# Fixed experts' round: the gather and the products taken by halves of the channels, and the order in which its weight slots are handed on

## The chip, the cores and the metric

One core of a Trainium2 chip runs the whole program. The metric is the device time of one launch, in microseconds (us); lower is better. The kernel before takes 1513.57 us, the median of three runs.

## The reference, cut to what matters

Two layers of a decoder with 512 tokens of 1024 channels. Each layer has a dense part (projections, three token mixers, output projection, LayerNorm) and then a mixture of 32 experts, of which each token uses two:

```python
for l in range(DEPTH):                      # DEPTH = 2
    ...                                     # token mixers, projection, layer_norm
    ffn = hierarchical_moe(x, ...)
    x = layer_norm(ALPHA * x + ffn, ...)

def run_block(args):                        # rows of one expert
    rows, e = args
    xb = x_pad[rows]
    hdn = silu(xb @ w_gate[e]) * (xb @ w_up[e])     # 1024 -> 512
    return hdn @ w_down[e]                          # 512 -> 1024
```

Every expert has three matrices of 2 MB in f32 ("gate", "up", "down"), so a layer reads 192 MB of expert weights.

## The kernel before

**Rounds.** In `moe` (from line 1312) the experts are taken in 13 rounds of 128 token slots. Round 0 is the *fixed* round: experts 0 and 16 of the kernel's numbering, 64 slots each, known before the routing. Rounds 1 to 12 hold two or three of the other 30 experts each, sorted by how many tokens they got, so their weights can be loaded only after the routing.

**A round on TensorE (PE).** `gather` (line 1320) builds the tokens of a round, channels on the partitions: the activations are multiplied by a matrix of ones and zeros (token to slot), in 16 matmuls for a *quarter*, that is for two of the eight blocks of 128 channels (line 1330). ACT (line 1341) and DVE (line 1339) copy one block each from PSUM to `xg`, with gain and bias. With n = 1 it builds one round, with n = 2 two rounds at a time. `hidden` (line 1364) multiplies the eight blocks k = 0 to 7 of `xg` by "gate" and "up" (line 1370); it can call *fillers*, other work put between its products, after every odd k. `act` (lines 1382, 1383) applies silu on ACT and the product on DVE, `turn` (lines 1389, 1390) transposes the result, `down` (line 1401) multiplies it by "down". `gated` (lines 1411, 1412) weighs the rows, `spread` (lines 1419, 1424, 1426) adds them to the tokens.

**The masks.** `gating`, `gating_all` and `tokens` (lines 1241 to 1284) compute each token's weights and slots on DVE, with two exponentials on ACT. `gates(r)` (line 1295) makes round r's matrix on DVE in 11 instructions: eight of line 1302, one of line 1306, and two (lines 1307, 1308) that write the ones and zeros into `fa` and an f16 copy, which `gather` reads. There are two places for them, for odd and for even rounds; the fixed round's lie in the place of round 1. `by_slot(r)` transposes the weights of round r on TensorE (line 1352, four transposes); DVE reads the result twice (lines 1354, 1355). For round 0 the weights come from a product on POOL (line 1599).

**Slots and the weight stream.** Weights lie in SBUF slots of 1 MB, half a matrix each: half 0 holds the channel blocks 0 to 3 of "gate" or "up", half 1 the blocks 4 to 7. `drop` (line 363) returns the slots of one or more matrices to the free list: first the half 0 of each matrix named, then the half 1 of each. `feed` (line 319) takes the next loads of a fixed order, puts each in the next free slot and issues it on SyncE (SP), line 357. SyncE works through its program in order, so it stands at a load until TensorE has read the slot's last contents, with all later loads behind it.

**Order.** From line 1590 on, PE, SP, DVE, ACT and POOL run in the order in which the program is written. Around the change it is, per layer: `feed` (five slots are free), the gather of the fixed round, gating and token counts, `gates(1)`, the products of the fixed round with `by_slot(0)` as the fourth filler, `feed`, `gates(2)`, `counts`, `act`, half the gather of rounds 1 and 2, `turn`, the other half, `by_slot(1)`, `down` of the fixed round. The products of the fixed round go half by half already: k = 0 to 3 of "gate", k = 0 to 3 of "up", then k = 4 to 7 of each. Its slots come back matrix by matrix: "gate" half 0, "gate" half 1, "up" half 0, "up" half 1 (two slots each).

Of the kernel before, what the change touches and what calls it, by code (L numbers as in the profile page):

```python
# [48 lines left out]
def rounds():  # L49

    kinds = list(KINDS)
    caps = [c for k in kinds for c in SIZES[k]]
    assert len(caps) == NF

    order = sorted(range(NF), key=lambda n: -caps[n])
    place = {n: j for j, n in enumerate(order)}
    r, n = [], 0
    for k in kinds:
        at, members = 0, []
        for c in SIZES[k]:  # L60
            members.append((place[n], at, at + c))
            at += c
            n += 1
        r.append(members)
    return r


ROUNDS = rounds()
# [4 lines left out]
def columns(members):  # L73

    w = 64 if all((b - a) % 64 == 0 for _, a, b in members) else 32
    return [(e, c, c + w) for e, (_, a, b) in enumerate(members) for c in range(a, b, w)]
# [86 lines left out]
class Trunk:  # L163
# [1147 lines left out]
    def moe(self, l):  # L1311
# [4 lines left out]
        xg = flat(f[:, 0:4, :]).rearrange("p (k s) -> p k s", k=8)  # L1316
# [3 lines left out]
        def gather(quarters=range(4), n=2):  # L1320

            w = 128 * n
            for kk in quarters:
                ps = self.t()
                for j in range(2):
                    k = 2 * kk + j
                    i = 0
                    for src, one in ((x1h, oh), (x1l, self.oh16)):
                        for t in range(NT):
                            nc.tensor.matmul(  # L1330
                                ps[:, w * j : w * j + w], src[:, k, 128 * t : 128 * t + 128],
                                one[:, 0:n, t, :], start=(i == 0), stop=(i == 2 * NT - 1),
                            )
                            i += 1
                for j in range(2):
                    k = 2 * kk + j
                    src = ps[:, w * j : w * j + w]
                    if j:
                        nc.vector.tensor_scalar(xg[:, k, 0:w], src, gain(k), bias(k), OP.mult, OP.add)  # L1339
                    else:  # L1340
                        nc.scalar.activation(xg[:, k, 0:w], src, AF.Identity, bias=bias(k), scale=gain(k))  # L1341

        def gate_of(r):
            return self.sm.tile([128, 1], F32, tag="gv", name="gv")

        def by_slot(r):

            gv = gate_of(r)
            gt = self.gt[:, (r - 1) % 2, :]
            ps = self.t()  # L1350
            for t in range(NT):
                nc.tensor.transpose(ps[:, 128 * t : 128 * t + 128], gt[:, 128 * t : 128 * t + 128], self.ident)
            oT = fa[:, 2 + r % 2, :]
            nc.vector.tensor_scalar(oT, ps, 0.0, None, OP.is_gt)
            nc.vector.tensor_reduce(gv, ps, AX.X, OP.add)
            return oT, gv

        def members(r):
            return len(ROUNDS[r - 1]) if r else len(FIXED)

        def weights(r, *names):
            return [self.loaded[(l, n, r, e)] for n in names for e in range(members(r))]

        def hidden(pss, w, xs, blocks, fill=(), parts=((0, 8),)):

            fill = list(fill)
            for m, part in [(m, part) for part in parts for m in range(len(w))]:
                for k in range(*part):
                    for e, a, b in blocks:
                        nc.tensor.matmul(  # L1370
                            pss[m][a:b, :], xs[:, k, a:b], w[m][e][:, k, :],
                            start=(k == 0), stop=(k == 7),
                        )
                    if k % 2 == 1 and fill:
                        fill.pop(0)()
# [52 lines left out]
        halves = [(0, 0, 64), (1, 64, 128)]  # L1428
# [113 lines left out]
        def release(r, *names):  # L1542
            for n in names:
                self.drop(*((l, n, r, e) for e in range(members(r))))

        def first(r, fill=(), keep=0):

            pss = [self.g(), self.g()]
            a = (r - 1) % 2 if r else 0
            xs = xg[:, :, 128 * a : 128 * a + 128]  # L1550
            if r:
                for m, n in enumerate(("gate", "up")):
                    if m:
                        self.feed()
                    hidden(pss[m:], [weights(r, n)], xs, columns(ROUNDS[r - 1]), fill[4 * m : 4 * m + 4])
                    release(r, n)
            else:
                w = [weights(r, n) for n in ("gate", "up")]
                hidden(pss, w, xs, halves, fill, ((0, 4), (4, 8)))
                release(r, "gate", "up")  # L1560
            if keep == 1:
                spare.append(self.free.pop())
            held = [self.free.pop() for _ in range(4 if keep == 4 else 0)]
            self.feed()
            self.free.extend(held)
            return pss
# [10 lines left out]
        def spreads(r, oT, y):  # L1577
            s = 1.0 if r else ALPHA
            return [lambda t=t, hf=hf: spread(oT, y[hf], t, hf, s) for t, hf in every]
# [10 lines left out]
        with self.manual(ET.PE, ET.SP):  # L1590

            self.known = l
            self.feed()
            gather(n=1)
            self.gating()
            self.gating_all()
            oh0 = oh[:, 0, :, :].bitcast(F32)
            gt0 = self.gt[:, 1, :].rearrange("p (t s) -> p t s", t=NT)
            nc.gpsimd.tensor_tensor(
                out=gt0, in0=oh0, in1=self.Gp.unsqueeze(2).broadcast_to([128, NT, 128]), op=OP.mult  # L1600
            )
            self.tokens()
            self.gates(1)
            nxt = []
            pss = first(0, [lambda: None] * 3 + [lambda: nxt.extend(by_slot(0))])
            self.gates(2)
            self.counts()
            nc.gpsimd.tensor_copy(self.cnt[:, 64:96], self.perm)
            h = act(pss)
            self.fb = self.half("y", FR, "Y")[0]  # L1610
            gather((0, 1))
            turn(h, hT)
            gather((2, 3))
            oT, gv = nxt
            nxt = by_slot(1)
            steps = spreads(0, oT, second(0, gv))

            for r in range(1, NR + 1):
                last = r == NR
                more = r % 2 == 0 and not last  # L1620
                counts = (0, 2, 0, 2, 0, 2, 0, 2)
                if row_steps:
                    counts = (0, 3, 0, 3, 0, 3, 0, 3)
                    steps = [f for n, st in enumerate(row_steps) for f in (*steps[2 * n : 2 * n + 2], st)]
                    row_steps = []
                if more:
                    self.gates(r + 1)
                    self.gates(r + 2)
                some, rest = several(steps, counts)
                h = act(first(r, some, 1 if r == NR - 2 else 4 if r == SLOW else 0))  # L1630
                oT, gv = nxt
                for step in rest:
                    step()
                if more:
                    gather((0, 1))
                elif not last:
                    nxt = by_slot(r + 1)
                turn(h, hT)
                if more:
                    gather((2, 3))  # L1640
                    nxt = by_slot(r + 1)
                if last:

                    nc.scalar.activation(f[:, 6, 0:1], self.eps, AF.Sqrt)
                if r == NR - 2:

                    tags = (self.x1t, *spare)
                    self.EF = [self.take(n, ty, t) for n, ty, t in (("E", F32, self.mht), ("qg", FR, tags))]
                    tabs, row_steps = lnrows()
                if r == SLOW:  # L1650
                    slow()
                    self.feed()
                if not last:
                    steps = spreads(r, oT, second(r, gv))
# [4 lines left out]
        def finish(t, hf):  # L1659
# [4 lines left out]
        fill = [  # L1664
            lambda: gated(pss[0], gv, 0),
            lambda: [finish(t, 0) for t in (0, 1)],
            lambda: [finish(t, 0) for t in (2, 3)],
        ]
        wl = self.loaded[(l, "last")].t
        n = 4 // members(NR)  # L1670
        w = lambda e, hf, j: wl[(4 * hf + j) // n][:, n * e + j % n, :]
        pss = [self.g(), self.g()]
# [163 lines left out]
```

## Time and profile before

| | |
|---|---|
| median of three runs | 1513.57 us (1512.85 to 1513.63) |
| the profiled execution's own time | 1514.36 us |
| its span (first to last instruction) | 1512.7 us |
| PE busy | 1362.2 us, 90% |
| DVE busy | 689.1 us, 46% |
| ACT busy | 395.2 us, 26% |
| POOL busy | 153.1 us, 10% |
| read from HBM | 441.45 MB, 293 GB/s over the span |

How to read it: busy times are averages over unlike stages, so the share of the whole span says little of one stage. Times in the rows are microseconds from the start of the span. A row of the timeline gives the start, the length from the first to the last of the merged instructions, the engine, the line of the kernel, the operation, what it writes and reads, its shape, and how many instructions were merged; in square brackets, if the engine stood idle before it, for how long and what ended that. A row of busy times by stretch gives the stretch, its length, the busy time of PE, PEld (weight loads into the array), DVE, ACT and POOL with their counts of instructions, then the granted TensorE clock (1.00 is 2.4 GHz, 0.50 is 1.2 GHz), the share of the DMA engines that was busy, and GB/s.

### The profile page before, as it was taken

To read this page: it belongs to the slowest core of one execution; us is meant where nothing else is said; L and a number is where in the kernel's file an instruction comes from. 1 tells how busy PE (TensorE), PEld (TensorE's weight loads), DVE (VectorE), ACT (ScalarE), POOL (GpSimd) and SP (SyncE) were. 2 spreads that over 40 slices of the span, in tenths; PEclk is the share of its full clock that TensorE was granted. 3 is DMA by queue.
4 is the path that set the end of the run, shared out by engine and by line. 5 is a ranking of instruction groups with operands and counts; after the bars stand their busy time and mean duration, and the time that the engine had idled before them with its cause. 6 is when DMAs were issued, how large, how long until landed. Compare 5 with 4: busy or idle time off the path is not lost. (4 is left out here: it accounts for less than half of the span.)

```text
span 1512.7 us, 22662 instructions
## 1 busy us (share of the span) xinstructions
PE 1362.2 (90%) x8836; PEld 755.1 (50%) x8837; DVE 689.1 (46%) x1540; ACT 395.2 (26%) x720; POOL 153.1 (10%) x188
## 2 busy tenths in 40 slices
PE   8999997899998988999699998979999989889994
PEld 7876576534343434343378665866343424343431
DVE  4347758524423242422553676585344242424225
ACT  5446544111010101011364555341110101010112
POOL 1112205100000000000141221050000000000001
PEclk9999999899999999999899998988999999999997
DMA  9410250799999999999911025408999999999994
GB/s 346 143 56 1 102 205 28 306 381 420 420 419 422 420 421 412 420 422 412 382 65 59 1 82 189 149 29 321 389 420 420 419 421 421 421 413 421 420 408 166
DMA packets 84550, 445.15 MB, mean 294 GB/s; under 512 B 8080, under 2 KB 14352, under 8 KB 36816
## 3 DMA queue, kind: packets, MB, share of 16 engines
q1 hardware_dynamic: 83184, 440.15, 72.5%
q0 software_dynamic: 960, 2.90, 0.6%
q8 instruction: 74, 1.21, 0.3%
q10 hardware_dynamic: 288, 0.52, 0.1%
q14 instruction: 44, 0.36, 0.1%
HBM read 441.45 MB, written 2.10 MB: 293 GB/s over the span
## 5 line engine op out<-in xcount | busy, mean ns | idle before, releaser
L1370 PE MATMUL g<-w,f 128*32 128x512 f32 (+1 forms) x3072 | 399.6, 595 | 13.7 <-DMA w<-expert_w_up 9.4
L1370 PEld LDWEIGHTS g<-w,f 128*32 128x32 f32 (+1 forms) x3072 | 120.8, 112 | 248.1 <-issue 202.4
L1401 PE MATMUL g<-w,f 128*32 128x512 f32 (+1 forms) x1536 | 211.6, 653 | 29.2 <-ACT f L1390 10.1
L1424 DVE TENSOR_TENSOR X<-X,s 128x512 f32<-128x512 f32 x176 | 113.0, 683 | 256.7 <-PE s L1419 256.7
L1401 PEld LDWEIGHTS g<-w,f 128*32 128x32 f32 (+1 forms) x1536 | 58.3, 121 | 161.7 <-issue 131.2
L1412 DVE SCALAR_TENSOR_TENSOR y<-g,gv,y 128x512 fp32r<-128x512 f32 x52 | 38.9, 750 | 212.1 <-ACT y L1411 209.8
L1419 PE MATMUL s<-y,fa 128*128 128x512 f32 x416 | 126.7, 425 | 6.4 <-DVE X L1424 3.5
L1419 PEld LDWEIGHTS s<-y,fa 128*128 128x128 f32 x416 | 70.1, 189 | 103.8 <-issue 71.9
L1411 ACT ACTIVATE y<-g,gv 128x512 fp32r<-128x512 f32 x52 | 35.5, 687 | 215.7 <-PE g L1401 215.7
L1330 PE MATMUL t<-fa,mh 128*128 128x256 f32 (+1 forms) x448 | 79.0, 298 | 8.9 <-ACT f L1390 8.8
L1341 ACT ACTIVATE f<-t,pp 128x256 f32<-128x256 f32 (+1 forms) x56 | 30.7, 549 | 206.7 <-PE t L1330 206.7
L1339 DVE TENSOR_SCALAR f<-t,pp 128x256 f32<-128x256 f32 (+1 forms) x56 | 29.4, 525 | 93.1 <-ACT f L1341 93.1
L1330 PEld LDWEIGHTS t<-fa,mh 128*128 128x128 f32 x448 | 61.3, 191 | 15.4 <-ACT f L1390 11.7
L1330 PE MATMUL t<-f,x1l 128*128 128x256 f16 (+1 forms) x448 | 64.9, 267 | 0.0
L1382 ACT ACTIVATE f<-g 128x512 f32<-128x512 f32 x26 | 15.6, 599 | 183.1 <-PE g L1370 183.1
L1530 POOL DMA_DIRECT2D rows<-ln_gain x2 | 1.1, 548 | 614.2 <-DMA w<-expert_w_gate 307.2
L1390 ACT COPY f<-t 128x512 f32<-128x512 f32 x26 | 15.2, 585 | 167.7 <-PE t L1389 167.7
L404 POOL TENSOR_TENSOR X<-X,f 128x512 f32<-128x512 f32 x32 | 40.5, 1296 | 87.9 <-DVE x1l L948 82.4
L404 POOL TENSOR_TENSOR X<-X,E 128x512 f32<-128x512 f32 x11 | 16.3, 1486 | 306.2 <-ACT X L1696 154.6
L701 ACT ACTIVATE f<-f,nm 128x128 f32<-128x128 f32 (+3 forms) x64 | 35.7, 558 | 43.7 <-POOL nm L700 42.9
L371 DVE TENSOR_TENSOR fa<-w,fa 128x512 fp32r<-128x512 f32 (+1 forms) x36 | 31.3, 877 | 32.0 <-ACT fa L370 31.9
L700 POOL TENSOR_SCALAR nm<-mx 128x1 f32<-128x1 f32 x64 | 22.3, 352 | 180.6 <-DVE mx L697 119.0
(338 smaller groups left out, 2165.5 us busy)
## 6 DMA issues: line engine op xcount, KB each, us to landing
w<-expert_w_gate SPq DMA_DIRECT2D x128, 1024.0 KB, 19.8
w<-expert_w_up SPq DMA_DIRECT2D x128, 1024.0 KB, 19.8
w<-expert_w_down SPq DMA_DIRECT2D x116, 1024.0 KB, 19.8
w<-w_in SPq DMA_DIRECT2D x20, 1024.0 KB, 13.6
w<-expert_w_down SPq DMA_DIRECT2D x48, 256.0 KB, 5.3
w<-w_out SPq DMA_DIRECT2D x8, 1024.0 KB, 5.3
X<-x SPq DMA_DIRECT2D x4, 512.0 KB, 5.9
w<-w_in SPq DMA_DIRECT2D x4, 512.0 KB, 8.2
```

The costliest lines, as they stand in the source:

```text
L371: self.nc.vector.tensor_sub(lo, src, hi.bitcast(F32))
L404: e.tensor_tensor(out=x, in0=x, in1=row[:, 512 * h : 512 * h + 512], op=op)
L701: nc.scalar.activation(p, p, AF.Exp, bias=nm, scale=0.125, accum_out=den)
L1330: nc.tensor.matmul(ps[:, w * j : w * j + w], src[:, k, 128 * t : 128 * t + 128], one[:, 0:n, t, :], start=(i == 0), stop=(i == 2 * NT - 1),)
L1339: nc.vector.tensor_scalar(xg[:, k, 0:w], src, gain(k), bias(k), OP.mult, OP.add)
L1341: nc.scalar.activation(xg[:, k, 0:w], src, AF.Identity, bias=bias(k), scale=gain(k))
L1370: nc.tensor.matmul(pss[m][a:b, :], xs[:, k, a:b], w[m][e][:, k, :], start=(k == 0), stop=(k == 7),)
L1401: nc.tensor.matmul(pss[hf][a:b, :], hT[:, 128 * j + a : 128 * j + b], part(e, hf, j), start=(j == 0), stop=(j == 3),)
L1411: nc.scalar.mul(yh, ps, gv)
L1412: nc.vector.scalar_tensor_tensor(yl, ps, gv, yh.bitcast(F32), OP.mult, OP.subtract)
L1419: nc.tensor.matmul(ps, oT[:, 128 * t : 128 * t + 128], y[q], start=(q == 0), stop=(q == 1))
L1424: nc.vector.tensor_add(x, x, ps)
```

## The change

The fixed round is begun by halves of the channels. The first two quarters of its gather are followed at once by the products of blocks 0 to 3 (`start`, first call). The gating and the token counts follow, then the other two quarters, `gates(1)`, and the products of blocks 4 to 7 (`start`, second call), with `by_slot(0)` as the third filler of that call. One `drop` of all four matrices returns the slots as "gate" half 0, "up" half 0, "gate" half 1, "up" half 1. `first` now serves rounds 1 to 12 alone.

```diff
+        def start(pss, part, fill=()):
+
+            w = [weights(0, n) for n in ("gate", "up")]
+            hidden(pss, w, xg[:, :, 0:128], halves, fill, (part,))
+
         def first(r, fill=(), keep=0):
 
             pss = [self.g(), self.g()]
-            a = (r - 1) % 2 if r else 0
+            a = (r - 1) % 2
             xs = xg[:, :, 128 * a : 128 * a + 128]
-            if r:
-                for m, n in enumerate(("gate", "up")):
-                    if m:
-                        self.feed()
-                    hidden(pss[m:], [weights(r, n)], xs, columns(ROUNDS[r - 1]), fill[4 * m : 4 * m + 4])
-                    release(r, n)
-            else:
-                w = [weights(r, n) for n in ("gate", "up")]
-                hidden(pss, w, xs, halves, fill, ((0, 4), (4, 8)))
-                release(r, "gate", "up")
+            for m, n in enumerate(("gate", "up")):
+                if m:
+                    self.feed()
+                hidden(pss[m:], [weights(r, n)], xs, columns(ROUNDS[r - 1]), fill[4 * m : 4 * m + 4])
+                release(r, n)
...
             self.known = l
             self.feed()
-            gather(n=1)
+            gather((0, 1), 1)
+            pss = [self.g(), self.g()]
+            start(pss, (0, 4))
             self.gating()
             self.gating_all()
...
             self.tokens()
+            gather((2, 3), 1)
             self.gates(1)
             nxt = []
-            pss = first(0, [lambda: None] * 3 + [lambda: nxt.extend(by_slot(0))])
+            start(pss, (4, 8), [lambda: None] * 2 + [lambda: nxt.extend(by_slot(0))])
+            self.drop(*((l, n, 0, e) for n in ("gate", "up") for e in range(members(0))))
+            self.feed()
             self.gates(2)
             self.counts()
```

## Rows read from the trace of the kernel before

**Rows 1.** The page's head.

```profile
span 1512.7 us, 22662 instructions
```

**Rows 2.** Busy times by stretch, first layer, around the fixed round and after it.

```profile
284.00:294.00 10.00, 10.00 (x50) 3.35 (x46) 9.58 (x29) 1.88 (x2) 0.42 (x2) 1.00 0.91 325
...
306.00:318.00 12.00, 12.00 (x84) 3.86 (x84) 2.69 (x4) 1.26 (x2) 0.00 (x0) 1.00 0.82 292
...
330.00:720.00 390.00, 357.45 (x2602) 151.29 (x2601) 137.77 (x273) 41.30 (x68) 1.06 (x2) 0.97 1.01 419
```

**Rows 3.** The chain that ended last: start, length, what; one piece.

```profile
1366.56 19.77 DMA w<-expert_w_gate
```

**Rows 4.** SyncE's timeline, and issues with size and us to landing, each below its own.

```profile
291.04 0.33 SPq L357 DMA_DIRECT2D w<-expert_w_up  x1
...
295.05 0.33 SPq L357 DMA_DIRECT2D w<-expert_w_down  x1
w<-expert_w_down SPq DMA_DIRECT2D x1, 1024.0 KB, 13.8
...
307.68 0.33 SPq L357 DMA_DIRECT2D w<-expert_w_down  x1
w<-expert_w_down SPq DMA_DIRECT2D x1, 1024.0 KB, 4.9
...
314.67 0.33 SPq L357 DMA_DIRECT2D w<-expert_w_down  x1
```

**Rows 5.** SyncE's waits, 295 to 330 us: total, times, longest.

```profile
SPq L357 <- PE g L1401: 15.0, 2, 12.1
```

**Rows 6.** TensorE's timeline around the fixed round.

```profile
276.71 0.64 PE L1330 MATMUL t<-fa,mh 128*128 128x128 f32 x4
...
279.76 7.09 PE L1370 MATMUL g<-w,f 128*64 128x512 f32 x32
286.78 0.65 PE L1352 MATMUL t<-ident,gt 128*128 128x128 f32 x4
287.37 7.09 PE L1370 MATMUL g<-w,f 128*64 128x512 f32 x32
294.52 0.74 PE L1330 MATMUL t<-fa,mh 128*128 128x256 f32 x4
...
311.00 3.64 PE L1370 MATMUL g<-w,f 128*32 128x512 f32 x32
```

**Rows 7.** VectorE's timeline over the same time.

```profile
277.77 0.41 DVE L1339 TENSOR_SCALAR f<-t,pp 128x128 f32<-128x128 f32 x1 [1.25 <-ACT f L1341]
...
280.75 0.17 DVE L1246 TENSOR_TENSOR f<-f,rs 128x16 f32<-128x16 f32 x1
...
286.29 1.12 DVE L1302 TENSOR_SCALAR gt<-tab,ur,rs 128x128 f32<-128x128 f32 x4
...
289.94 0.68 DVE L1354 TENSOR_SCALAR fa<-t 128x512 fp32r<-128x512 f32 x1
...
291.14 1.10 DVE L1302 TENSOR_SCALAR gt<-tab,ur,rs 128x128 f32<-128x128 f32 x4
...
294.03 0.43 DVE L1307 TENSOR_SCALAR fa<-gt 128x512 fp32r<-128x512 f32 x1
```

**Rows 8.** VectorE's timeline in the second layer, the mask of round 2.

```profile
1048.22 0.43 DVE L1307 TENSOR_SCALAR fa<-gt 128x512 fp32r<-128x512 f32 x1
```

**Rows 9.** Busy times by stretch, around waits of TensorE.

```profile
943.00:946.70 3.70, 1.22 (x7) 0.53 (x6) 0.65 (x1) 1.53 (x2) 0.72 (x2) 1.00 0.47 161
946.80:950.10 3.30, 3.30 (x18) 2.68 (x17) 1.22 (x3) 1.48 (x3) 1.47 (x3) 0.50 0.24 36
...
328.90:335.70 6.80, 4.90 (x40) 2.28 (x43) 3.08 (x5) 0.58 (x1) 0.00 (x0) 1.00 1.02 423
```

**Rows 10.** TensorE's timeline: sixteen like matmuls, first at the upper level, then the lower.

```profile
259.93 2.03 PE L1114 MATMUL g<-ident 128*128 128x128 f32 x16
...
270.17 3.78 PE L1114 MATMUL g<-ident 128*128 128x128 f32 x16
```

## The prediction

> **What bounds the kernel now.** I read the page's head first, then the busy times by stretch, then the issues on SyncE's queue, and last the timelines of TensorE (PE) and VectorE (DVE) around the change. The profiled execution spans 1512.7 us [rows 1]. By stretch, the expert rounds of the first layer (330 to 720 us) hold the DMA engines at a share of 1.01 and 419 GB/s: there the weight stream is full, and a 1 MB load takes 2.5 us (1.049 MB over 419 GB/s). Two stretches before that are not full: 284 to 294 us moves 325 GB/s, 306 to 318 us 292 GB/s [rows 2]. Late in the second layer the chain that ended last still runs through a weight load of 19.77 us that was queued behind others [rows 3]. So whatever moves the start of the full stream moves the end of the layer by as much, and the question is what starts it.
>
> SyncE's queue answers. Loads are issued as slots come free. The second load of "up" of round 1 is issued at 291.04, the first of "down" at 295.05, landing 13.8 us later, at 308.85. The next goes out at 307.68 and lands 4.9 us later, the shortest time of these rows: nothing was queued before it. One more leaves at 314.67 [rows 4]; of SyncE's waits between 295 and 330 us 15.0 us are for the products of line 1401 [rows 5]. 307.68 is inside those products of the fixed experts (they end before 311.00), 314.67 is the end of the first products of round 1, which start at 311.00 [rows 6]. So from 295 us on TensorE hands out the slots, the DMA engines have gaps, and the full stream starts when TensorE has read the first half of round 1's gate weights. TensorE itself goes from one step to the next without a wait at 276.71, 279.76, 286.78, 287.37 and 294.52 [rows 6]. At 294.52 two things meet: its products of the fixed round have run 7.02 us from 287.37, to 294.39, and DVE has finished the mask of round 2 (line 1307, 294.03 + 0.43 = 294.46), which the gather of rounds 1 and 2 reads [rows 6, 7]. DVE is as late as TensorE can bear, already.
>
> **The change, part by part.**
>
> *Slots and their order.* Today SyncE stands at the slots of gate half 1 while those of up half 0 are free. Afterwards the first half's products begin with the gather's first half done, near 276.71 rather than at 279.76, and end near 276.71 + 7.02 = 283.73; four slots come free by then and are taken in that order. Eight loads are issued as before, none added. This can fill at most the gap of 284 to 294 us: 10 us x (1 - 325/419) = 2.2 us a layer. But the next load waits for line 1401, with or without it: 308.85 moves to 306.6 at best, and the load of 307.68 still leaves when TensorE releases it. The 2.2 us become a longer gap at 307 us. I count nothing; the bounds are 0 and a gain of 2.2 us.
>
> *The gather's second half* (two of four quarters) goes behind the first half's products. TensorE's sum is the same: 3.05 us (279.76 - 276.71) move from before to after the 7.02 us. First half to 283.73, gather to 286.78, second half from there: gate until 290.3, the end at 286.78 + 7.02 + 0.59 (the transposes, 287.37 - 286.78) = 294.39, as now. Its two evictions on ACT and two on DVE (0.41 us each) now stand behind the gating and the token counts on DVE. Those take 286.29 - 280.75 = 5.54 us and can start after the eviction of 277.77, at 278.18, so DVE is free at 283.7, when the gather's second half has only begun [rows 7]. Cost nothing; with DVE over 1.5 us later a stall of that excess would show. POOL's product of line 1599 and the two exponentials of ACT come earlier by 2.6 us with the gating; nothing waits for them.
>
> *gates(1)* follows those evictions. The eviction that ends at 278.18 is of the quarter that ended at 276.71, 1.5 us before; so here 286.78 + 1.5 = 288.3 at the latest. It takes 289.94 - 286.29 = 3.65 us [rows 7], to 291.9. It also overwrites the one-hots of the fixed round, which the gather has read by then. Cost nothing, as long as it ends before the transposes of the next step (292.70).
>
> *by_slot(0) is the step that costs.* Its four transposes stood behind the first half's products, at 286.78. Now they are the third filler of the second half: behind gate k = 5, gate k = 7 and up k = 5, that is behind 6 of 8 steps, 286.78 + 0.75 x 7.02 = 292.05. They end at 292.70 (0.65 us busy), and DVE's line 1354 reads them then, at about 292.75; today it starts at 289.94, when gates(1) lets it. DVE runs its program in order, so behind this wait stand line 1355, the eleven instructions of gates(2), the four of counts, the product of line 1383 and the next evictions. From line 1354 to line 1302 is 291.14 - 289.94 = 1.20 us, from there to the end of line 1307 294.46 - 291.14 = 3.32 us: 292.75 + 1.20 + 3.32 = 297.27, and TensorE's gather starts 0.06 us later, at 297.33 rather than 294.52. **2.8 us a layer**, in which TensorE has nothing else to do. The following steps (turn, the second gather, the fixed "down") hang on that gather, so 307.68 and 314.67 go later by the same 2.8 us, and the full stream with them. The second layer repeats it: line 1307 starts at 1048.22 [rows 8], 754.19 us after its twin. Two layers: 5.6 us.
>
> *The clock after the wait.* A TensorE wait of 2.8 us at this place has no row. The nearest ones: 943.00 to 946.70 us, with 2.5 us of its 3.7 idle, and then 0.50 of the clock (the lower of its two levels, 1.2 GHz) from 946.80 to 950.10; on the other side 328.90 to 335.70, idle for 1.9 us in two pieces, at 1.00 (2.4 GHz) all through [rows 9]. Sixteen like matmuls take 3.78 us at the lower level and 2.03 at the upper, 1.86 times as long [rows 10]. So 3.3 us at the lower level do 1.8 us of work and cost 1.5 us, on a TensorE that has no slack there. Bounds 0 (the clock stays, or falls within the wait) and 3.0 us (two such stretches); I take 1.4 us, as the new wait is nearest to that of 943 and some of the low stretch may lie in the wait itself. Two layers: 2.8 us.
>
> **Sum.** 5.6 + 2.8 = 8.4 us. The profiled execution took 1514.36 us in all (1.7 us around its span) and would take 1522.8; it lies 0.8 us above the median of the runs, so the median goes from 1513.57 to **1522.0 us**.
>
> **The rivals.**
>
> *The same wait, the clock stays up*: 5.6 us, 1519.2. For it speaks 328.90 to 335.70; against it that those 1.9 us were broken by work and the new wait isn't.
>
> *Faster: the weight stream itself sets the pace.* If the load landing at 308.85 set the later ones, the 2.2 us closed at 284 to 294 would carry through: 4.4 us less, 1509.1. For that the next load must be queued while the last is still moving, by 308.85 - 4.9 = 303.95; it is issued at 307.68 and would be 5.9 us late after the change. The Trainium skill, "Perfetto Trace Analysis", section "Identifying Performance Opportunities", advises to take the most-contended engine and close the gaps on it; by that advice the gap on the DMA engines is the one to close, and the change closes it. The row of 306 to 318 us shows the other gap, which TensorE opens, and that one grows.
>
> *No change: the wait is covered.* If something later took the 2.8 us back, 1513.6. It would need slack in the stream after 330 us of that size; a share of 1.01 over 390 us leaves none. It would also come if DVE finished gates(2) by 294.5 all the same, that is with line 1354 done as early as now; the order on DVE excludes it.
>
> *Worse*: two low-clock stretches after each wait, 2 x (2.8 + 3.0) = 11.6 us, 1525.2.
>
> That the slots aren't handed on as said can be ruled out: one drop of four tiles returns their first halves, then their second.
>
> **How the numbers follow.** Wait and fallen clock 0.58; wait alone 0.18; no change 0.10; faster 0.10; worse 0.04. The likeliest case's own range is 1519.0 to 1523.8. The range takes in the no-change case, with the 0.6 us by which the runs of before differ, and the worse case's foot: 1513.0 to 1525.0; faster and most of worse are left out. A measurement here can tell about 0.2%, 3.0 us, from no change. So faster 0.10, same 0.10, slower 0.80.
>
> **What would show it.** In the changed kernel: gate loads issued near 280 us and up loads near 284; a wait of TensorE of about 2.9 us before the gather at 294.4, released by DVE's fa (line 1307); line 1354 preceded by DVE idle that ends with the transposes; the load of 307.68 at 310.5 or later, with a wider gap before it; every landing after 330 us later by 3 to 4.5 us. The forecast is wrong if the gather starts by 295 us, or if the stream after 330 us is not later although it starts late.

## The result and the profile after

The changed kernel takes 1523.10 us (median; 1521.81 to 1525.11) where the kernel before takes 1515.01 us on the same chip: a ratio of **1.0058 [1.0047, 1.0069]**, so slower by more than the 0.2% that can be told from no change. One of the six runs of the kernel before was slow (1584.94 us), and the ratio, which leaves it out, is not the quotient of the two medians. On the 1513.57 us of the table the forecast of 1522.0 us is a ratio of 1.0056. The profiled execution of the changed kernel took 1522.66 us; the page's head answers to [rows 1]:

```profile
span 1521.0 us, 22672 instructions
```

That is 8.3 us more span. Where it lies shows first in the busy times by stretch of the changed kernel (columns as in [rows 2]); the last two rows stand around TensorE's new wait:

```profile
284.00:294.00 10.00, 10.00 (x68) 5.28 (x68) 5.22 (x15) 2.79 (x4) 0.00 (x0) 1.00 1.02 423
...
306.00:318.00 12.00, 12.00 (x81) 5.34 (x84) 3.69 (x6) 2.39 (x4) 0.00 (x0) 1.00 0.35 109
...
330.00:720.00 390.00, 356.31 (x2588) 150.69 (x2586) 137.82 (x273) 41.29 (x68) 1.06 (x2) 0.97 1.01 420
...
294.90:298.80 3.90, 1.15 (x11) 1.04 (x10) 3.76 (x15) 0.00 (x0) 0.00 (x0) 1.00 1.00 418
298.90:302.20 3.30, 3.30 (x17) 2.74 (x17) 0.81 (x2) 0.56 (x1) 0.00 (x0) 0.50 1.00 417
```

The change does what it says: the first of the two gaps in the weight stream is closed, 423 GB/s where [rows 2] had 325. But the second gap is wider, 109 GB/s where it was 292, and the full stream behind it is as full as before. The Trainium skill, "Perfetto Trace Analysis", section "Identifying Performance Opportunities", advises to look for the gaps on the most contended engine and for what blocks the work behind each. This case bears out that the second step is needed: the gap at 284 to 294 us was closed (423 GB/s), the one behind which the next load waits for TensorE grew (109 GB/s), and the kernel is 0.6% slower.

SyncE's issues in the changed kernel say why (each with its size and time to landing below it where it counts), against [rows 4]:

```profile
295.53 0.33 SPq L357 DMA_DIRECT2D w<-expert_w_down  x1
w<-expert_w_down SPq DMA_DIRECT2D x1, 1024.0 KB, 11.6
...
312.44 0.33 SPq L357 DMA_DIRECT2D w<-expert_w_down  x1
w<-expert_w_down SPq DMA_DIRECT2D x1, 1024.0 KB, 5.3
...
319.44 0.33 SPq L357 DMA_DIRECT2D w<-expert_w_down  x1
```

The first load of "down" lands at 295.53 + 11.6 = 307.1, 1.7 us earlier than before. The next is issued at 312.44, 4.8 us later than before, and finds empty queues (5.3 us to landing); the one after it at 319.44, also 4.8 us later. SyncE's wait for TensorE's line 1401 in that time grew from the 15.0 us of [rows 5] to 19.3:

```profile
SPq L357 <- PE g L1401: 19.3, 2, 16.4
```

TensorE's timeline in the changed kernel, against [rows 6]. The number in brackets is the idle time ahead of the row and what ended it.

```profile
277.19 7.09 PE L1370 MATMUL g<-w,f 128*64 128x512 f32 x32
284.21 0.66 PE L1330 MATMUL t<-fa,mh 128*128 128x128 f32 x4
...
287.11 5.37 PE L1370 MATMUL g<-w,f 128*64 128x512 f32 x24
292.41 0.66 PE L1352 MATMUL t<-ident,gt 128*128 128x128 f32 x4
293.00 1.94 PE L1370 MATMUL g<-w,f 128*64 128x512 f32 x8
297.68 0.74 PE L1330 MATMUL t<-fa,mh 128*128 128x256 f32 x4 [2.75 <-DVE fa L1307]
...
303.08 0.60 PE L1389 MATMUL t<-ident,f 128*128 128x128 f32 x4
...
1055.32 0.74 PE L1330 MATMUL t<-fa,mh 128*128 128x256 f32 x4 [2.75 <-DVE fa L1307]
```

VectorE's timeline in the changed kernel, against [rows 7]:

```profile
291.40 0.42 DVE L1308 TENSOR_SCALAR f<-gt 128x512 f16<-128x512 f32 x1
293.10 0.69 DVE L1354 TENSOR_SCALAR fa<-t 128x512 fp32r<-128x512 f32 x1 [1.28 <-PE t L1352]
294.31 1.10 DVE L1302 TENSOR_SCALAR gt<-tab,ur,rs 128x128 f32<-128x128 f32 x4
...
297.20 0.43 DVE L1307 TENSOR_SCALAR fa<-gt 128x512 fp32r<-128x512 f32 x1
```

VectorE is through with gates(1) at 291.82 and stands 1.28 us for the transposes (line 1352), which TensorE reaches only at 292.41. Then it runs line 1354 and gates(2), to 297.63. TensorE, done with the products at 294.9, waits 2.75 us for that, in both layers. Then the clock drops to 0.50 for 3.3 us, and from the gather to the next step (line 1389) pass 303.08 - 297.68 = 5.40 us. In the kernel before the row of line 1389 is

```profile
298.30 0.60 PE L1389 MATMUL t<-ident,f 128*128 128x128 f32 x4
```

which makes 298.30 - 294.52 = 3.78 us. So the 4.8 us of the first layer are 3.16 up to the gather (297.68 - 294.52: the wait of 2.75, and 0.41 by which the products end later, having begun at 277.19) and 1.62 at the lower clock. The second layer does the same, and the piece of the chain that stood at 1366.56 in [rows 3] starts 8.2 us later:

```profile
1374.78 19.64 DMA w<-expert_w_gate
```

### The profile page after: what moved, and what is told of

It reads as the page before. It is cut to its first block, busy times and chain, and to the rows that moved or that the text cites. A ratio compares the mean times of both kernels' runs of the same rounds, so it can differ in the third digit from the quotient of the medians.

```text
span 1521.0 us, 22672 instructions
## 1 busy us (share of the span) xinstructions
PE 1364.8 (90%) x8836; PEld 757.1 (50%) x8837; DVE 688.6 (45%) x1540; ACT 395.4 (26%) x720; POOL 153.3 (10%) x188
```

## Experiments

Theory: VectorE works in program order, the late transposes hold up gates(2), TensorE waits for its mask, and the lower clock follows. Rivals: the new order of slots or the halves themselves cost the time; or the wait alone does it and the clock nothing. Every ratio is to the kernel before on the same chip.

**1. The changed kernel, transposes early.**

```diff
-            gather((2, 3), 1)
-            self.gates(1)
-            nxt = []
-            start(pss, (4, 8), [lambda: None] * 2 + [lambda: nxt.extend(by_slot(0))])
+            nxt = by_slot(0)
+            gather((2, 3), 1)
+            self.gates(1)
+            start(pss, (4, 8))
```

> The changed kernel with by_slot(0) put in front of the gather's second half (its transposes near 284 us, DVE's two reads near 285 to 286 us, where DVE stands idle for 2.4 us in the changed kernel); halves, slot order and all else as changed. Theory (DVE's order: the wait for the transposes holds gates(2) back): gates(1) then runs from about 288.7 to 292.3, gates(2) reaches the end of line 1307 near 295.7, TensorE's wait before the gather falls from 2.75 us to 0.6 to 0.9 us a layer, the clock stays at 1.00 after it, and the time is 1.001 of before (1.000 to 1.002). Rival (the halves, the slot order or the loads taken earlier cost the time): it stays at 1.006.

Measured: 1516.2 us, 1.0013 [1.0004, 1.0022]. TensorE's timeline of this kernel:

```profile
295.58 0.74 PE L1330 MATMUL t<-fa,mh 128*128 128x256 f32 x4 [0.92 <-DVE fa L1307]
```

and its busy times in the stretch from that wait on:

```profile
294.70:298.80 4.10, 3.22 (x27) 2.99 (x28) 2.68 (x9) 0.56 (x1) 0.00 (x0) 1.00 1.01 422
```

The wait is 0.92 us, the clock stays at 1.00, and two waits of 0.92 us are 1.8 us of 1515, or 0.0012: what is left of the loss. Halves and slot order are both still in.

**2. The kernel before, transposes late alone** (in the fixed round's first, which is one piece there; slots in the old order).

```diff
-            pss = first(0, [lambda: None] * 3 + [lambda: nxt.extend(by_slot(0))])
+            pss = first(0, [lambda: None] * 6 + [lambda: nxt.extend(by_slot(0))])
```

> The kernel before with one thing changed: by_slot(0) is the seventh filler of the fixed round's products (behind up k = 5) and not the fourth; gather, slot order and loads as before. Theory: the same wait of 2.7 to 2.8 us before the gather near 294.4, released by DVE's fa of line 1307, in both layers, and 1.0055 of before (1.0045 to 1.0065). Rival (halves or slots cost the time): 1.000.

Measured: 1521.69 us, 1.0047 [1.0033, 1.0060]. TensorE's timeline of this kernel:

```profile
297.25 0.74 PE L1330 MATMUL t<-fa,mh 128*128 128x256 f32 x4 [2.75 <-DVE fa L1307]
```

VectorE's:

```profile
292.68 0.69 DVE L1354 TENSOR_SCALAR fa<-t 128x512 fp32r<-128x512 f32 x1 [2.59 <-PE t L1352]
```

and the busy times after the wait:

```profile
298.50:301.70 3.20, 3.20 (x17) 2.64 (x16) 0.79 (x2) 0.56 (x1) 0.00 (x0) 0.50 0.99 417
```

One moved step alone makes the same wait to the hundredth, the same clock, and most of the loss; its interval overlaps that of the whole change.

**3. The kernel before, slot order alone.**

```diff
-                    release(r, "gate", "up")
+                    self.drop(*((l, n, 0, e) for n in ("gate", "up") for e in range(members(0))))
```

> The kernel before with the slot order alone: one drop of the fixed round's four matrices, so gate half 0, up half 0, gate half 1, up half 1. Theory (TensorE hands out the slots that start the full stream): two loads of up leave near 287 rather than 291 us, the gap of the DMA engines at 284 to 294 us shrinks, the one at 306 to 312 us grows by as much, and the time is 1.000 of before (0.999 to 1.001). Rival (the weight stream sets the pace): up to 2.2 us a layer, 0.997 to 0.9985.

Measured: 1515.07 us, 1.0002 [0.9992, 1.0011]. By stretch:

```profile
284.00:294.00 10.00, 9.93 (x49) 3.50 (x46) 9.62 (x31) 1.88 (x2) 0.00 (x0) 1.00 0.95 369
306.00:318.00 12.00, 12.00 (x88) 3.62 (x84) 2.70 (x4) 1.26 (x2) 0.00 (x0) 1.00 0.80 280
```

Read with care: in this execution the layer's start was some 1.1 us early, so the rates of the windows are not only the edit's. The time is: no change.

**4. Filling the wait, to keep the clock up.** Matmuls on the identity, of no use to the result, run behind the changed kernel's second start; first twenty, then, with 11 in place of 20, eleven.

```diff
+            self.warm(20)
```

> The changed kernel with 20 matmuls of 128 columns on the identity (2.5 us at the upper clock level) where TensorE waits before the gather of rounds 1 and 2. Theory (the wait costs its length and then a low clock): the gather starts at the same time behind DVE's line 1307, but at 1.00 of the clock; it takes 3.8 us up to turn and not 5.4 us, and the time is 1.0037 of before (1.003 to 1.0045), 3 us less than the change. Rival (the lower clock is covered by other waits): 1.0058 as changed.

> As the run with 20 matmuls in TensorE's wait, but with 11: the 20 made 40 instructions and 4.7 us, 1.7 us longer than the wait, and delayed the gather. Theory: 22 instructions end before DVE's line 1307, the gather starts when DVE lets it, at 1.00 of the clock, takes 3.8 us up to turn and not 5.4 us, and the time is 1.0037 of before (1.003 to 1.0048). Rival (the lower clock is covered by other waits): 1.0058 as changed.

Measured: 1523.16 us, 1.0065 [1.0051, 1.0079] with twenty, a miss; 1521.04 us, 1.0037 [1.0024, 1.0050] with eleven. TensorE's timeline with twenty:

```profile
293.49 4.73 PE L1114 MATMUL g<-ident 128*128 128x128 f32 x40
297.98 0.72 PE L1330 MATMUL t<-fa,mh 128*128 128x256 f32 x4
```

with eleven:

```profile
293.69 2.72 PE L1114 MATMUL g<-ident 128*128 128x128 f32 x22
296.51 0.73 PE L1330 MATMUL t<-fa,mh 128*128 128x256 f32 x4
...
300.29 0.60 PE L1389 MATMUL t<-ident,f 128*128 128x128 f32 x4
```

and the busy times of the gather's stretch, with eleven:

```profile
296.50:300.20 3.70, 3.69 (x32) 3.40 (x33) 1.97 (x7) 0.56 (x1) 0.00 (x0) 1.00 1.02 423
```

Twenty calls made forty instructions and 4.73 us, longer than the wait they were to fill. With eleven the gather starts when its mask is ready, the clock stays at 1.00, and gather to turn takes 300.29 - 296.51 = 3.78 us, as before the change. The wait is still there, only filled. So of the loss of 0.0058 some 0.0037 (5.6 us) are the wait and the rest, 0.0021 (3 us), the clock. By times alone this split isn't shown: the two intervals overlap, the twelve runs with eleven lie between 1516.13 and 1522.87 us, and the trace is of one of the fastest (1517.48). The traces of the two kernels say it more firmly, for one execution of each. By their rows the lower clock costs 5.40 - 3.78 = 1.62 us a layer. And from the fixed round's gather to the start of the second layer's dense part (line 450) the changed kernel takes 747.20 - 273.73 = 473.47 us, the one with eleven 744.73 - 272.69 = 472.04, which is 1.43 less. The first two rows are of the changed kernel, the others of the one with eleven:

```profile
273.73 1.09 PE L1330 MATMUL t<-fa,mh 128*128 128x128 f32 x4
747.20 1.12 PE L450 MATMUL t<-ident,X 128*128 128x128 f32 x4 [4.08 <-DVE X L1707]
272.69 1.09 PE L1330 MATMUL t<-fa,mh 128*128 128x128 f32 x4
744.73 1.12 PE L450 MATMUL t<-ident,X 128*128 128x128 f32 x4 [4.07 <-DVE X L1708]
```

**5. Halves without a wait.** Two tries at keeping halves and slot order with VectorE in time. The first puts nine instructions of gates(1) ahead of by_slot(0):

```diff
...
-            gather((2, 3), 1)
-            self.gates(1)
-            nxt = []
-            start(pss, (4, 8), [lambda: None] * 2 + [lambda: nxt.extend(by_slot(0))])
+            self.gates(1, mask=False)
+            nxt = by_slot(0)
+            gather((2, 3), 1)
+            self.mask_of(1)
+            start(pss, (4, 8))
```

The second splits gates(1) around the two quarters, behind the transposes:

```diff
...
+            nxt = by_slot(0)
+            self.gates(1, 1)
+            gather((2,), 1)
+            self.gates_sum(1)
+            gather((3,), 1)
+            self.gates_mask(1)
+            start(pss, (4, 8))
```

> The changed kernel with DVE's work put in time: the nine instructions of gates(1) that touch no one-hots, and by_slot(0), run ahead of the gather's second half, and only lines 1307 and 1308 of gates(1) behind it. Halves and slot order stay. Theory (TensorE hands out the slots; the halves cost nothing and bring nothing): no wait of TensorE before the gather of rounds 1 and 2, loads of up near 284 us, the first load of down landing 1.5 to 2 us earlier, the next one still issued near 307.7, and 1.000 of before (0.999 to 1.001). Rival (the loads taken earlier are worth what they close): 0.997 to 0.9985.

> The changed kernel with DVE in time, as the run before that tried it, but with by_slot(0) read by DVE ahead of gates(1): there TensorE waited 2.0 us for the PSUM bank of the transposes, which DVE read only behind nine instructions of gates(1). Now by_slot(0) is read at 284.7 to 285.9, then come eight instructions of gates(1), the eviction of k = 5, line 1306, the eviction of k = 7 and the mask. Theory (TensorE hands out the slots; the halves cost nothing and bring nothing): no wait of TensorE over 0.5 us from 276 to 298 us, and 1.000 of before (0.999 to 1.0012), though the first load of down lands 1.5 to 2 us earlier. Rival (the halves cost something of their own): 1.003 or more; rival (the loads taken earlier are worth what they close): 0.997 to 0.9985.

Measured: 1524.08 us, 1.0052 [1.0033, 1.0070], a miss; then 1515.10 us, 1.0004 [0.9994, 1.0013]. TensorE's timeline in the first (there line 1337 is the gather, 1377 the products, 1362 VectorE's second reading of the transposes):

```profile
287.85 0.91 PE L1337 MATMUL t<-fa,mh 128*128 128x128 f32 x4 [2.01 <-DVE gv L1362]
...
290.45 9.26 PE L1377 MATMUL g<-w,f 128*64 128x512 f32 x32
```

The transposes ran early, but VectorE read them only behind its nine instructions, and the gather's last quarter waited for that reading, which by the releaser is for the PSUM bank that it holds: the wait had moved, not gone. The clock fell after it too, and the products of 7.09 us took 9.26. The second try, by stretch:

```profile
284.00:294.00 10.00, 9.86 (x68) 5.18 (x66) 9.27 (x30) 2.79 (x4) 0.00 (x0) 1.00 1.02 421
306.00:318.00 12.00, 12.00 (x84) 3.86 (x84) 2.69 (x4) 1.26 (x2) 0.00 (x0) 1.00 0.71 241
```

No TensorE wait is left there, the first gap is as closed as in the changed kernel, and the time is that of the kernel before: the 0.96 MB gained in the first stretch (10 us x 96 GB/s) are lost again, 0.61 MB in the second (12 us x 51 GB/s) and 0.48 MB in the 12 us between (385 GB/s, 425 before). This is the change without its fault, and it is worth nothing, because the next load still goes out when TensorE lets it (307.55; 307.68 before).

**6. Freeing the slots earlier.** If TensorE hands out the slots, its order has to change. Round 1's gate products go ahead of the fixed round's down; in a second version also ahead of the turn, with the gather in one piece. The second's core, against the kernel before (the first leaves gather, turn and by_slot(1) where they were):

```diff
-            gather((0, 1))
-            turn(h, hT)
-            gather((2, 3))
-            oT, gv = nxt
-            nxt = by_slot(1)
-            steps = spreads(0, oT, second(0, gv))
+            gather()
+            kept, after, h0 = nxt, [], h
+            nxt = []
+            def down0():
+                turn(h0, hT)
+                nxt.extend(by_slot(1))
+                steps = spreads(0, kept[0], second(0, kept[1]))
...
+                    if m and mid:
+                        fill = mid()
```

> The kernel before with one step of TensorE moved: the gate products of round 1 stand before the fixed round's down products and not behind them. The same work in all, but three slots come free near 307.6 us and three more near 311, where there were one and one. Theory (the full stream starts when TensorE has read round 1's first gate half): the third load after 300 us lands near 317.5 and not at 319.5, every later one 2 us earlier, in both layers: 0.9974 of before (0.9965 to 0.9985). Rival (something else paces the layer, TensorE's own sum of work for one): 1.000.

> As the run with the gate products of round 1 before the fixed round's down, and further: all four quarters of the gather of rounds 1 and 2 without a break, then round 1's gate products, and turn and by_slot(1) behind these, ahead of down. Gate products then start near 302 us, slots come free near 305.7, the stream has hardly a gap behind 308.85. Theory: the third load after 300 us lands near 316.3, 3.2 us earlier than before, in both layers, and TensorE loses its wait of 0.75 us for a PSUM bank: 0.9958 of before (0.9945 to 0.997). Rival (TensorE's sum of work paces the layer): 0.999 to 1.000.

Measured: 1512.26 us, 0.9979 [0.9967, 0.9991]; 1507.48 us, 0.9947 [0.9928, 0.9966]. The second, by stretch:

```profile
284.00:294.00 10.00, 10.00 (x50) 3.46 (x48) 9.58 (x30) 1.88 (x2) 1.26 (x2) 1.00 0.91 338
306.00:318.00 12.00, 11.72 (x82) 4.23 (x76) 1.29 (x2) 0.59 (x1) 0.00 (x0) 1.00 1.01 415
```

and the piece of its chain that answers to [rows 3]:

```profile
1362.40 19.78 DMA w<-expert_w_gate
```

The first gap is left as it was, the second is closed, and the chain is 4.2 us early: the opposite of the change, with the opposite sign. Up to 0.75 us a layer of the gain may be a wait of TensorE that the second version no longer has. It stands ahead of the gather's later half in the kernel before, and in the first version too, which gains without losing it:

```profile
299.65 0.74 PE L1330 MATMUL t<-fa,mh 128*128 128x256 f32 x4 [0.75 <-ACT f L1390]
```

**7. Both together**, the halves of 5 and the order of 6, and a second run of each beside the other on one chip:

> That kernel with round 1's gate products first (all of the gather, gate products, turn, by_slot(1), down), the order that gave 0.9947 on the kernel before. With slots free at 307 us the stream has no gap left there, so a stream that is ahead at 295 us stays ahead. Theory: the gap of 284 to 294 us closes and the load issued near 307 lands 1.5 us earlier than in that run, 3 us in two layers: 0.9927 of before (0.991 to 0.9945). Rival (the loads taken earlier never matter): 0.9947.

> The kernel with round 1's gate products first, once more, on the same chip as the next run, so that the two can be compared. 0.9947 of before as in its first run (0.993 to 0.9965).

> The same with the halves. In the traces of the first runs the third load after 300 us lands 44.9 us after the layer's first gate issue (314.99 - 270.11) and 46.1 us without the halves (318.70 - 272.59), 1.2 us earlier a layer. If that carries through, 2.4 us less than the run beside it: 0.0016 lower in the ratio, about 0.9931. Rival (the loads taken earlier never matter): the same median as the run beside it within 1 us.

Measured: 1506.71 us, 0.9943 [0.9927, 0.9958]; then 1508.07 us, 0.9962 [0.9949, 0.9976], without the halves, and 1507.71 us, 0.9954 [0.9940, 0.9967], with them. The kernel with both, first run, by stretch:

```profile
284.00:294.00 10.00, 9.86 (x63) 4.79 (x60) 9.10 (x31) 2.79 (x4) 0.00 (x0) 1.00 1.01 422
306.00:318.00 12.00, 11.76 (x76) 4.00 (x72) 2.05 (x4) 2.07 (x4) 0.00 (x0) 1.00 0.98 407
```

Now both gaps are closed. Either version beats both kernels. The gain expected of the halves did not come: 0.9931 was forecast for the second run with them, 2.4 us below the run beside it, and the medians differ by 0.4 us, as the rival had it. The intervals overlap, so whether the halves add anything to the new order stays open.

## Why the prediction was right

- *Slots and their order, counted at nothing*: right. Experiments 3 and 5 (second try) show it by time; the first load of "down" landed at 307.1, 0.5 us short of the best case (306.6), and the next was not earlier for it. The rival "the weight stream itself sets the pace" fell with that: its gap was closed and nothing came through.
- *The gather's second half and gates(1), at nothing*: right in this order. gates(1) was done at 291.82 (worked out: 291.9), ahead of the transposes.
- *by_slot(0), 2.8 us a layer*: right in place, cause and size. Line 1354 at 293.10 (292.75 forecast), line 1307's end at 297.63 (297.27); both 0.35 us late, and the layer's first products were 0.48 us later than the forecast's start (277.19, 276.71). The wait itself is 2.75 us in both layers. Experiment 1 takes the loss away with the wait, experiment 2 brings most of it back with this one step.
- *The clock, 1.4 us a layer out of 0 to 3.0*: right, a little low. 1.62 us in the first layer, 1.61 in the second (1055.32 to 1060.71, less 3.78); the second run of experiment 4 gives some 3 us for both. "The same wait, the clock stays up" is that run, 1.0037.
- *Sum*: 8.4 us forecast, 8.3 by the spans. That they agree to 0.1 us is luck, for it isn't split as forecast (4.2 us a layer). The release by line 1401 is 4.8 us late in the first layer. Of that 4.37 us are left where the second layer's dense part begins (line 450), and 3.27 at the first matmuls of its fixed round; from there to the end of the span the second layer adds 5.0. So both fixed rounds cost more than forecast, and 1.1 us came back in the dense part between them, which the change doesn't touch: it takes 285.13 us in the trace before and 284.03 in the changed kernel's, and between 282.72 and 285.86 in the fourteen traces of this case. The first two rows are of the kernel before, the others of the changed kernel:

```profile
742.83 1.12 PE L450 MATMUL t<-ident,X 128*128 128x128 f32 x4 [4.08 <-DVE X L1702]
1027.96 0.98 PE L1330 MATMUL t<-fa,mh 128*128 128x128 f32 x4
...
747.20 1.12 PE L450 MATMUL t<-ident,X 128*128 128x128 f32 x4 [4.08 <-DVE X L1707]
1031.23 1.09 PE L1330 MATMUL t<-fa,mh 128*128 128x128 f32 x4
```

- *The stream behind the wait*: the load of 307.68 was to go out at 310.5 or later, and goes out at 312.44. Every landing after 330 us was to be 3 to 4.5 us later. That was put too low: the issues there are 4.8 us later in the first layer (334.68 rather than 329.90), and late in the second the chain's piece is 8.2 us later. Of the loads of "up", forecast near 284 us, one goes out at 281.45 and the next two from 284.30 on.

## What to carry to other kernels

Before a step is moved, list what stands behind its result on the engine that reads it: on an engine that works in order, one instruction that waits holds up everything after it, and the price shows on another engine. A gap in a saturated stream is worth closing only if the next transfer isn't released by something else; look for the engine that frees the buffers and move its work, as in 6. An engine that has just enough time is best watched at both of its ends: in 5 the same lateness came back as a PSUM bank that wasn't free.

## What the runs showed of the hardware that was not expected

The clock fell behind shorter waits too, and behind one of them for longer. In the first try of 5 a TensorE wait of 2.01 us was followed by 6.8 us at 0.50 of the clock,

```profile
288.00:294.80 6.80, 6.80 (x28) 3.53 (x30) 3.68 (x13) 1.74 (x2) 0.00 (x0) 0.50 1.01 423
```

twice as long as after the wait of 2.75 us. In the second layer of the same kernel the wait was 1.73 us, and 3.4 us at 0.50 followed:

```profile
1049.20:1052.60 3.40, 3.40 (x18) 2.30 (x19) 0.78 (x3) 1.25 (x2) 0.00 (x0) 0.50 1.01 427
```

So the length of the wait alone doesn't tell what it costs; what else does, no run here shows. After 0.92 us (experiment 1) it stayed at 1.00, and likewise where 2.72 us of useless matmuls filled the wait. And a call of a matmul on the f32 identity counts as two instructions in the trace: 20 calls 40, 11 calls 22, at 0.12 us each.
